# x^T and the forget columns side by side in DRAM, the first eight transfers feeding eight forget blocks k by k

## The chip, the cores and the metric

The kernel runs on one core of a Trainium2 chip. The metric is the device time of one execution in microseconds. The tensor engine is PE (its weight loads PEld), the vector engine DVE, the scalar engine ACT, GpSimd POOL; SP is the queue from which most transfers are issued. KB and MB in the text are 1024 and 1024 x 1024 bytes.

## The reference

One hybrid decoder layer for 256 tokens and 1024 channels. The stage that the change touches is the input projection, and of it the 1024 forget columns; the rest is cut.

```python
proj = jnp.einsum('bsd,dn->bsn', x, w_in)          # 256 x 1024 by 1024 x 9216
hq, hf, hi, hg, mq, mk, mv, gate_logits = jnp.split(proj, offsets, axis=-1)
# hf: columns 1024..2047, 8 heads of 128
o_a = hgrn2_mixer(hq, hf, hi, lb)                  # log_f and k = (1 - lb) * sigmoid(-hf), ...
y_b = moba_attention(rope(mq), rope(mk), mv)       # causal softmax within 256 tokens
mixed = (g_a * (y_a @ w_branch_a) + g_b * (y_b @ w_branch_b)) @ w_out
x = layer_norm(alpha * x + mixed)
return layer_norm(alpha * x + swiglu(x))
```

## The kernel before

**Products.** Every large product is made of three: each operand is split into a high part in the rounded type fp32r and the remainder, and high x high, low x high and high x low are added up in PSUM. `split` (L135) does this with a cast on ACT and a subtraction on DVE; `stage` (L143) does the same to a tile of weights that SP brings from DRAM (`raw` to `wh` and `wl`). A weight tile has 128 x 2048 elements, 1 MB. `plan` (L71) lists all weight tiles in the order in which they are used, and the host lays them into `wts` in that order. `fetch` (L165) takes the next tile and stages as many as three ahead; `prefetch` stages without taking.

**Layouts.** In products with the feature on the partitions ("feat") the weights are the stationary operand, 128 x 128 per k and block, and x^T (1024 channels as 8 pieces k of 128 partitions, 256 tokens) moves: `feat_steps` (L213) issues the three matmuls of 256 columns for each k. A "block" f is 128 columns of the projection; `feat_pair` (L205) takes a tile of two blocks and all eight k and finishes one block after the other. "tok" tiles hold four k and 512 columns.

**Order.** The instructions on PE, DVE and ACT in the block at L255 to L281 go out in the order in which they are written; SP's and those behind the block are ordered by the scheduler, which plays the program through on a model and gives each instruction its place when its inputs and buffers are there. Semaphores and slots are given out by it too: the pool `big` has 12 slots of 8 KB a partition (`slot`), which a tile holds from its first write to its last read; `wraw` has 3 buffers, `whi` and `wlo` 4 each, and in PSUM the pools `mm` and `aux` have 4 banks each.

**The first stage.** L256 to L265: a small activation, a tile of ones, and seven matmuls of ones (`warm`), which PE runs while the first data are under way. L266 to L273: for each k SP brings the x^T piece (128 x 256, 128 KB) and then four blocks' weights of that k (128 x 512, 256 KB, a quarter of a "tok" tile); ACT and DVE split each. `feat_first` (L221) then runs k by k over the four blocks f = 0..3, 12 matmuls a k, into four `aux` banks. L277 brings the tile of blocks 4 and 5 in two halves, L278 computes the lower bounds from the vector `vec`, L279 brings the tile of blocks 6 and 7, and `forget` (L248) evacuates blocks 0 to 3: two sigmoids on ACT (Kt and Fg) and one scaling on DVE. L282 to L287 run blocks 4 to 7 with `feat_pair` out of `mm` banks, one after the other, and evacuate them; the constants `cst` (960 KB) are brought behind the first of these pairs. Then come the query blocks hq (L288), the values hi, the output gates hg and the rest.

Of the kernel before, what the change touches and what calls it, by code (L numbers as in the profile page):

```python
# [10 lines left out]
F32 = mybir.dt.float32  # L11
F32R = mybir.dt.float32r
# [5 lines left out]
P = 128  # L18
T = 256
NT = T // P  # L20
D = 1024
KC = D // P
# [8 lines left out]
NEG = -1e30  # L31
LOOKAHEAD = 3
WARM = 7
EARLY = 4
HOLD_IN = 2
HOLD_DOWN = 3
# [34 lines left out]
def plan():  # L71

    tiles = []

    def add(w, k0, kn, c0, n, held=False):
        tiles.append((w, k0, kn, c0, n, held))

    def feat(w, c0, n):
        for c in range(c0, c0 + n, 256):
            add(w, 0, 8, c, 256)  # L80

    def tok(w, c0, n):
        for c in range(c0, c0 + n, 512):
            add(w, 0, 4, c, 512)
            add(w, 4, 4, c, 512)

    tok("w_in", 1024, 512)
    feat("w_in", 1536, 512)
    feat("w_in", 0, 1024)
    tok("w_in", 2048, 1024)  # L90
    feat("w_in", 3072, 1024)
    feat("w_in", 8192, 1024)
    feat("w_in", 7168, 1024)
    for c in range(2):
        feat("w_in", 5120 + c * 512, 512)
        feat("w_in", 4096 + c * 512, 512)
        tok("w_in", 6144 + c * 512, 512)
    feat("w_branch_a", 0, 1024)
    feat("w_branch_b", 0, 1024)
    for k in range(0, KC, 2):  # L100
        add("w_out", k, 2, 0, 1024)
    for j in range(0, NF, 2):
        add("w_ffn_in", 0, 8, j * P, 256, j < HOLD_IN)
        add("w_ffn_in", 0, 8, FF + j * P, 256, j < HOLD_IN)
    for k in range(0, NF, 2):
        add("w_ffn_down", k, 2, 0, 1024)
    return tiles


@with_exitstack  # L110
def hybrid_layer_kernel(ctx: ExitStack, tc, x, xT, vecs, wts, ln1_w, ln1_b, ln2_w, ln2_b, consts, out):
    nc = tc.nc
    pool = lambda name, bufs, **kw: ctx.enter_context(tc.tile_pool(name=name, bufs=bufs, **kw))
    cp = pool("cp", 1)
    wraw = pool("wraw", 3)
    whi = pool("whi", 4)
    wlo = pool("wlo", 4)
# [3 lines left out]
    mm = pool("mm", 4, space=PSUM)  # L121
    aux = pool("aux", 4, space=PSUM)

    def slot(name, dt=F32):
        return big.tile([P, 2048], dt, tag="s8", name=name)

    def r32(ap):
        return ap.bitcast(F32)


    loads = plan()
    ready = []
    state = {"next": 0}

    def split(dst_h, dst_l, src):  # L135
        nc.scalar.copy(dst_h, src)
        nc.vector.tensor_sub(dst_l, src, r32(dst_h))

    def ks_of(pieces):
        at = np.cumsum((0,) + tuple(pieces))  # L140
        return [slice(int(a), int(b)) for a, b in zip(at[:-1], at[1:])]

    def stage(pieces=None, eng=nc.vector):  # L143
        i = state["next"]
        if i >= len(loads):
            return
        state["next"] += 1
        _, _, k, _, _, held = loads[i]
        src = wts[i].rearrange("p (k c) -> p k c", k=k)
        view = lambda z: z.rearrange("p (k c) -> p k c", k=k)  # L150
        raw = view(wraw.tile([P, 2048], F32, tag="raw", name=f"raw{i}"))
        if held:
            h, l = view(slot(f"wh{i}", F32R)), view(slot(f"wl{i}", F32R))
        else:
            h = view(whi.tile([P, 2048], F32R, tag="h", name=f"wh{i}"))
            l = view(wlo.tile([P, 2048], F32R, tag="l", name=f"wl{i}"))
        for ks in ks_of(pieces or (k,)):
            nc.sync.dma_start(raw[:, ks, :], src[:, ks, :])
            nc.scalar.copy(h[:, ks, :], raw[:, ks, :])  # L159
            yield  # L160
            eng.tensor_sub(l[:, ks, :], raw[:, ks, :], r32(h[:, ks, :]))  # L161
            yield
        ready.append((h, l))

    def fetch(ahead=LOOKAHEAD):  # L165
        while state["next"] < len(loads) and len(ready) < 1 + ahead:
            list(stage())
        return ready.pop(0)
# [3 lines left out]
            list(stage())  # L172


    xTr = slot("xTr").rearrange("p (k t) -> p k t", k=KC)
    xTh = slot("xTh", F32R).rearrange("p (k t) -> p k t", k=KC)
    xTl = slot("xTl", F32R).rearrange("p (k t) -> p k t", k=KC)
    vec = cp.tile([P, 5 * H], F32, tag="vec", name="vec")
    cst = cp.tile([P, C_END], F32, tag="cst", name="cst")
# [25 lines left out]
    def feat_pair(name, ah=None, al=None):  # L205
        ah, al = (xTh, xTl) if ah is None else (ah, al)
        wh, wl = fetch()
        ps = mm.tile([P, 2, T], F32, tag="mm", name=name)
        for f in range(2):
            feat_steps(ps[:, f, :], wh, wl, f, ah, al, range(KC))  # L210
        return ps

    def feat_steps(ps, wh, wl, f, ah, al, ks, k0=0):  # L213
        wcol = slice(f * P, (f + 1) * P)
        for k in ks:
            kk = k0 + k
            nc.tensor.matmul(ps, wh[:, k, wcol], ah[:, kk, :], start=(kk == 0), stop=False)  # L217
            nc.tensor.matmul(ps, wh[:, k, wcol], al[:, kk, :], start=False, stop=False)  # L218
            nc.tensor.matmul(ps, wl[:, k, wcol], ah[:, kk, :], start=False, stop=(kk == KC - 1))  # L219

    def feat_first(pss, tiles):  # L221

        for q, (wh, wl) in enumerate(tiles):
            for k in range(4):
                for f, ps in enumerate(pss):
                    feat_steps(ps, wh, wl, f, xTh, xTl, (k,), 4 * q)

    def tok_chunk(name, evac):
        pss = [mm.tile([P, 512], F32, tag="mm", name=f"{name}_{t}") for t in range(NT)]
# [18 lines left out]
    def forget(h, ps):  # L248
        nc.scalar.activation(Kt[:, :, h, :], by_half(ps), AF.Sigmoid, scale=-1.0)
        nc.scalar.activation(Fg[:, :, h, :], by_half(ps), AF.Sigmoid)  # L250
        nc.vector.tensor_scalar(Fg[:, :, h, :], Fg[:, :, h, :], lb[:, H + h:H + h + 1], lb[:, h:h + 1],
                                op0=ALU.mult, op1=ALU.add)

    ET = mybir.EngineType
    with tc.manual_schedule(engines={ET.PE, ET.DVE, ET.Activation}):  # L255
        act = cp.tile([P, 2], F32, tag="act", name="act")  # L256
        nc.vector.memset(act, 0.0)
        nc.scalar.activation(act[:, 0:1], act[:, 1:2], AF.Exp)
        one = cp.tile([P, P], F32, tag="one", name="one")
        nc.vector.memset(one, 1.0)  # L260
        nc.scalar.copy(ones, one)
        warm = aux.tile([P, P], F32, tag="aux", name="warm")
        for _ in range(WARM):
            nc.tensor.matmul(warm, one, one, start=True, stop=True)
        nc.vector.memset(half, -0.5)  # L265
        for q in range(2):  # L266
            w = stage((1, 1, 1, 1))
            for k in range(4 * q, 4 * q + 4):
                nc.sync.dma_start(xTr[:, k, :], xT[:, k, :])
                split(xTh[:, k, :], xTl[:, k, :], xTr[:, k, :])  # L270
                next(w)
                next(w)
            list(w)  # L273
        nc.sync.dma_start(vec, vecs)
        hf0 = [aux.tile([P, T], F32, tag="aux", name=f"hf0{f}") for f in range(4)]
        feat_first(hf0, [ready.pop(0) for _ in range(2)])
        list(stage((4, 4)))  # L277
        lower_bounds()  # L278
        list(stage())  # L279
        for f in range(4):  # L280
            forget(f, hf0[f])  # L281
    for j in range(2, 4):  # L282
        ps = feat_pair(f"hf{j}")
        if j == 2:
            tc.keep_in_program_order(nc.sync.dma_start(cst, consts))
        for f in range(2):
            forget(2 * j + f, ps[:, f, :])  # L287
    for j in range(4):  # L288
        ps = feat_pair(f"hq{j}")
        sg = sm.tile([P, 2, T], F32, tag="sg", name=f"sgq{j}")  # L290
        nc.scalar.activation(sg, ps, AF.Sigmoid)
        for f in range(2):
            h = 2 * j + f
# [128 lines left out]
    for j in range(4):  # L422
        ps = feat_pair(f"hg{j}")
        sg = sm.tile([P, 2, T], F32, tag="sg", name=f"sgg{j}")
        nc.scalar.activation(sg, ps, AF.Sigmoid)
        for f in range(2):
            h = 2 * j + f
# [87 lines left out]
    for j in range(4):  # L515
        side.step()
        ps = feat_pair(f"za{j}", yah, yal)
# [5 lines left out]
    for j in range(4):  # L523
        ps = feat_pair(f"zb{j}", ybh, ybl)
# [45 lines left out]
    def row_parts(name, widths, n0=0):  # L570
        parts = []
        for i, (p, w) in enumerate(widths):
            parts.append((p.tile([P, w], F32, tag="aux" if p is aux else "mm", name=f"{name}{i}"), n0))
            n0 += w
        return parts
# [57 lines left out]
    pss = [row_parts(f"wo{t}", [(aux, 512)] * 2) for t in range(NT)]  # L633
    wb2 = bcast("wb2", ln2_w, ln2_b)
    with tc.manual_schedule(engines={ET.PE, ET.DVE, ET.Activation}):
        tiles = [(2 * q,) + fetch(0) for q in range(4)]
# [32 lines left out]

    for j in range(EARLY, NF, 2):  # L670
        pg = feat_pair(f"fg{j}", x1h, x1l)
# [4 lines left out]
        i, k = divmod(j, KC)  # L676
        split(ah[i][:, k:k + 2, :], al[i][:, k:k + 2, :], sg)

    pss = [row_parts("wd0", [(aux, 512)] * 2), row_parts("wd1", [(aux, 512), (aux, 256), (mm, 256)])]
    lhs = (lambda kk: ah[kk // KC][:, kk % KC, :], lambda kk: al[kk // KC][:, kk % KC, :])  # L680
    y = slot("y").rearrange("p (t d) -> p t d", t=NT)
    tiles = []
# [8 lines left out]
    layer_norm("n2", 1, pss[1], x1[:, 1, :], wb2, y[:, 1, :], store=out[P:T, :])  # L691


_INS = ['x', 'xT', 'vecs', 'wts', 'ln1_w', 'ln1_b', 'ln2_w', 'ln2_b', 'consts']


# [27 lines left out]
```

## Time and profile before

| | |
|---|---|
| median of 3 runs | 517.9 us (517.75 to 518.09) |
| profiled execution, device time | 517.71 us |
| its span, first to last instruction | 515.7 us |
| mean granted tensor engine clock | 0.997 |
| bytes moved | 91.73 MB, mean 178 GB/s |

The profile is of one execution. A row of the timeline has the start in us from the start of the span, the duration, the engine, the line, the operation, what it writes and reads, and in square brackets the idle time of its engine before it and what ended it. The end of a matmul is modelled, so the pace of PE is read from the starts of consecutive ones and not from the durations. A row of the windows has a stretch, its length, each engine's busy time with the count of its instructions, the granted clock, the busy share of the DMA engines, and what they moved in GB/s. In the chain that ended last, each step is followed back to what released it.

### The profile page before, as it was taken

The page shows a single profiled execution, that of the slowest core. Times are in us where ns is not written, and L with a number is a line of the kernel's source. Part 1 is how long each engine was busy: PE and PEld are TensorE (multiplying, and loading weights), DVE is VectorE, ACT ScalarE, POOL GpSimd, SP SyncE. Part 2 cuts the span into 40 slices and gives each one's busy share as a digit, 9 for nine tenths or more (in the row PEclk, how much of TensorE's full clock was granted, in tenths as well). Part 3 has the DMA queues.
Part 4 walks back from the last instruction along what each step waited for, and adds up shares of the span by engine and source line. Part 5 has one row for each costly group of instructions (what it writes and reads, how often), then busy time and mean ns, then how long its engine had stood idle before and what let it go on. Part 6 is the DMA issues. An engine that isn't in the chain of part 4 may idle for free.

```text
span 515.7 us, 8629 instructions
## 1 busy us (share of the span) xinstructions
PE 506.5 (98%) x3728; PEld 484.8 (94%) x3728; DVE 327.2 (63%) x351; ACT 236.1 (46%) x267; POOL 39.9 (8%) x33
## 2 busy tenths in 40 slices
PE   8999999999999999999999999999999999999994
PEld 7999889999999998998999988999999999988884
DVE  4677799997575444775772899555445454543436
ACT  5695355444354455656442553543443344324300
POOL 0000000000110162353010001000000000000000
PEclk9999999999999999999999999999999999999998
DMA  7988453343424555444575475055554455456002
GB/s 236 354 305 323 167 186 142 128 151 131 164 83 165 168 188 216 165 163 160 179 247 232 163 275 215 5 213 198 192 209 167 165 186 210 174 168 203 39 1 81
DMA packets 15573, 91.73 MB, mean 178 GB/s; under 512 B 1840, under 2 KB 2864, under 8 KB 5552
## 3 DMA queue, kind: packets, MB, share of 16 engines
q1 hardware_dynamic: 14688, 88.04, 47.5%
q0 software_dynamic: 848, 3.15, 1.9%
q8 instruction: 29, 0.48, 0.4%
q14 instruction: 8, 0.07, 0.0%
HBM read 90.13 MB, written 1.05 MB: 177 GB/s over the span
## 4 chain that ended last, share of the span: by engine, by line
PE 98%; DMA 1%; DVE 1%; issue 0%; DVEq 0%; ACT 0%; SPq 0%
PE wd L547 4%; PE wd L546 4%; PE wd L548 4%; PE fu L217 3%; PE fg L218 3%; PE fg L217 3%; PE fg L219 3%; PE fu L218 3%; PE fu L219 3%; PE sc L343 3%; PE hf L219 2%; PE hf L217 2%; PE hf L218 2%; PE mk L219 1%; PE hq L219 1%; PE hq L218 1%
## 5 line engine op out<-in xcount | busy, mean ns | idle before, releaser
L161 DVE TENSOR_TENSOR wl<-raw,wh 128x2048 fp32r<-128x2048 f32 (+2 forms) x88 | 186.6, 2122 | 123.1 <-ACT wh L159 122.7
L159 ACT CAST wh<-raw 128x2048 fp32r<-128x2048 f32 (+2 forms) x88 | 155.8, 1772 | 186.1 <-issue 50.3
L217 PE MATMUL fg<-x1h,wh 128*128 128x256 f32 x144 | 40.8, 284 | 0.0
L217 PE MATMUL fu<-x1h,wh 128*128 128x256 f32 x144 | 40.8, 284 | 0.0
L218 PE MATMUL fg<-x1l,wh 128*128 128x256 f32 x144 | 40.8, 283 | 0.0
L219 PE MATMUL fg<-x1h,wl 128*128 128x256 f32 x144 | 40.8, 283 | 0.0
L218 PE MATMUL fu<-x1l,wh 128*128 128x256 f32 x144 | 40.7, 283 | 0.0
L219 PE MATMUL fu<-x1h,wl 128*128 128x256 f32 x144 | 40.7, 283 | 0.0
L547 PE MATMUL wd<-wl,ah 128*128 128x512 f32 (+1 forms) x110 | 38.2, 348 | 0.0
L546 PE MATMUL wd<-wh,ah 128*128 128x512 f32 (+1 forms) x110 | 38.2, 347 | 0.0
L548 PE MATMUL wd<-wh,al 128*128 128x512 f32 (+1 forms) x110 | 38.1, 347 | 0.0
L218 PEld LDWEIGHTS fg<-x1l,wh 128*128 128x128 f32 x144 | 27.6, 192 | 0.0
L219 PEld LDWEIGHTS fg<-x1h,wl 128*128 128x128 f32 x144 | 27.6, 192 | 0.0
L217 PEld LDWEIGHTS fg<-x1h,wh 128*128 128x128 f32 x144 | 27.6, 192 | 0.0
L218 PEld LDWEIGHTS fu<-x1l,wh 128*128 128x128 f32 x144 | 27.6, 192 | 0.0
L219 PEld LDWEIGHTS fu<-x1h,wl 128*128 128x128 f32 x144 | 27.6, 192 | 0.0
L217 PEld LDWEIGHTS fu<-x1h,wh 128*128 128x128 f32 x144 | 27.6, 192 | 0.0
L546 PEld LDWEIGHTS wd<-wh,ah 128*128 128x128 f32 x110 | 20.8, 189 | 2.7
L548 PEld LDWEIGHTS wd<-wh,al 128*128 128x128 f32 x110 | 20.8, 189 | 2.7
L547 PEld LDWEIGHTS wd<-wl,ah 128*128 128x128 f32 x110 | 20.8, 189 | 2.6
L217 PE MATMUL hf<-xTh,wh 128*128 128x256 f32 x64 | 19.3, 301 | 1.0 <-ACT wh L159 1.0
L219 PE MATMUL hf<-xTh,wl 128*128 128x256 f32 x64 | 19.3, 302 | 0.0
(218 smaller groups left out, 1436.5 us busy)
## 6 DMA issues: line engine op xcount, KB each, us to landing
raw<-in_wts_dram SPq DMA_DIRECT2D x78, 1024.0 KB, 4.8
raw<-in_wts_dram SPq DMA_DIRECT2D x8, 256.0 KB, 5.0
xTr<-in_xT_dram SPq DMA_DIRECT2D x8, 128.0 KB, 4.7
raw<-in_wts_dram SPq DMA_DIRECT2D x2, 512.0 KB, 7.0
xr<-in_x_dram POOLq DMA_DIRECT2D x1, 1024.0 KB, 5.4
wb<-in_ln_w_dram POOLq DMA_DIRECT2D x2, 512.0 KB, 5.7
wb<-in_ln_b_dram POOLq DMA_DIRECT2D x2, 512.0 KB, 7.4
out_dram<-y SPq DMA_DIRECT2D x4, 256.0 KB, 2.1
```

Of the source, the lines that this page charges most:

```text
L159: nc.scalar.copy(h[:, ks, :], raw[:, ks, :])
L161: eng.tensor_sub(l[:, ks, :], raw[:, ks, :], r32(h[:, ks, :]))
L217: nc.tensor.matmul(ps, wh[:, k, wcol], ah[:, kk, :], start=(kk == 0), stop=False)
L218: nc.tensor.matmul(ps, wh[:, k, wcol], al[:, kk, :], start=False, stop=False)
L219: nc.tensor.matmul(ps, wl[:, k, wcol], ah[:, kk, :], start=False, stop=(kk == KC - 1))
L343: nc.tensor.matmul(ps[:, a, :], KL[:, h, :], later(Qt, n, h, 1), start=True, stop=True)
L546: nc.tensor.matmul(ps, lh(kk)[:, ts], wh[:, k, ns], start=(kk == 0), stop=False)
L547: nc.tensor.matmul(ps, lh(kk)[:, ts], wl[:, k, ns], start=False, stop=False)
L548: nc.tensor.matmul(ps, ll(kk)[:, ts], wh[:, k, ns], start=False, stop=(kk == ktot - 1))
```

## The change

x^T and the 1024 forget columns of `w_in` are concatenated on the host into `xw`, of shape 128 x 8 x 1280: for each partition and k, 256 values of x^T and 1024 weights stand in one row. Eight slots of `big` take one k each. SP issues nine transfers: for k = 0 the first 512 columns (x^T and two blocks' weights, 256 KB) and the other 768 (384 KB), then 640 KB for each further k; behind them `vec`. The four forget tiles leave the plan.

ACT and DVE split k by k: x^T, then the weights of all eight blocks of that k (for k = 0 in the parts 256 and 768 columns). The split weights of two k share a `whi` and a `wlo` buffer, so four of each are taken. The new `feat_first` runs, for k = 0 to 5, all eight blocks: first the 16 matmuls with the high weights, then the 8 with the low weights; for k = 0 blocks 0 and 1 go first (four and two), then blocks 2 to 7. `feat_last` runs k = 6 and 7 block by block, so that the blocks end one after the other. The eight banks are the four of `mm` (blocks 0 to 3) and the four of `aux` (4 to 7). Behind it come the lower bounds, one weight tile ahead, the evacuation of blocks 0 to 3, a second tile ahead, and that of 4 to 7; the constants are brought after these in the program. The memset of `one` stands ahead of that of `act`.

```diff
-    tok("w_in", 1024, 512)
-    feat("w_in", 1536, 512)
     feat("w_in", 0, 1024)
...
+    def feat_first(pss, k, wh, wl):
+
+        kk = k % 2
+        for fs in [(0, 1), range(2, 8)] if k == 0 else [range(8)]:
+            for f in fs:
+                wcol = slice(f * P, (f + 1) * P)
+                nc.tensor.matmul(pss[f], wh[:, kk, wcol], xTh[:, k, :], start=(k == 0), stop=False)
+                nc.tensor.matmul(pss[f], wh[:, kk, wcol], xTl[:, k, :], start=False, stop=False)
+            for f in fs:
+                wcol = slice(f * P, (f + 1) * P)
+                nc.tensor.matmul(pss[f], wl[:, kk, wcol], xTh[:, k, :], start=False, stop=False)
+
+    def feat_last(pss, wh, wl):
+
+        for f, ps in enumerate(pss):
+            feat_steps(ps, wh, wl, f, xTh, xTl, (0, 1), KC - 2)
...
+        first = [slot(f"xw{k}")[:, 0:T + D] for k in range(KC)]
+        for k in range(KC):
+            cut = [0, T + FIRST, T + D] if k == 0 else [0, T + D]
+            for c0, c1 in zip(cut[:-1], cut[1:]):
+                nc.sync.dma_start(first[k][:, c0:c1], xw[:, k, c0:c1])
+        nc.sync.dma_start(vec, vecs)
...
-        for q in range(2):
-            w = stage((1, 1, 1, 1))
-            for k in range(4 * q, 4 * q + 4):
-                nc.sync.dma_start(xTr[:, k, :], xT[:, k, :])
-                split(xTh[:, k, :], xTl[:, k, :], xTr[:, k, :])
-                next(w)
-                next(w)
-            list(w)
-        nc.sync.dma_start(vec, vecs)
-        hf0 = [aux.tile([P, T], F32, tag="aux", name=f"hf0{f}") for f in range(4)]
-        feat_first(hf0, [ready.pop(0) for _ in range(2)])
-        list(stage((4, 4)))
+        hf = [p.tile([P, T], F32, tag=tag, name=f"hf{f}")
+              for f, (p, tag) in enumerate([(mm, "mm")] * 4 + [(aux, "aux")] * 4)]
+        for i in range(KC // 2):
+            wh, wl = [p.tile([P, 2048], F32R, tag=tag, name=f"f{tag}{i}").rearrange("p (k c) -> p k c", k=2)
+                      for p, tag in ((whi, "h"), (wlo, "l"))]
+            for k in range(2 * i, 2 * i + 2):
+                cut = [0, FIRST, D] if k == 0 else [0, D]
+                split(xTh[:, k, :], xTl[:, k, :], first[k][:, 0:T])
+                for c0, c1 in zip(cut[:-1], cut[1:]):
+                    split(wh[:, k % 2, c0:c1], wl[:, k % 2, c0:c1], first[k][:, T + c0:T + c1])
+                if k < KC - 2:
+                    feat_first(hf, k, wh, wl)
+        feat_last(hf, wh, wl)
         lower_bounds()
-        list(stage())
-        for f in range(4):
-            forget(f, hf0[f])
-    for j in range(2, 4):
-        ps = feat_pair(f"hf{j}")
-        if j == 2:
-            tc.keep_in_program_order(nc.sync.dma_start(cst, consts))
-        for f in range(2):
-            forget(2 * j + f, ps[:, f, :])
+        prefetch(1)
+        for f in range(8):
+            forget(f, hf[f])
+            if f == 3:
+                prefetch(1)
+    tc.keep_in_program_order(nc.sync.dma_start(cst, consts))
```

More of the change, by code (lines that the diff above doesn't have):

```diff
@@ L33 @@
 WARM = 7
+FIRST = 256
 EARLY = 4
@@ L110, in hybrid_layer_kernel @@
 @with_exitstack
-def hybrid_layer_kernel(ctx: ExitStack, tc, x, xT, vecs, wts, ln1_w, ln1_b, ln2_w, ln2_b, consts, out):
+def hybrid_layer_kernel(ctx: ExitStack, tc, x, xw, vecs, wts, ln1_w, ln1_b, ln2_w, ln2_b, consts, out):
     nc = tc.nc
@@ L172, in prefetch @@
             list(stage())
-    xTr = slot("xTr").rearrange("p (k t) -> p k t", k=KC)
     xTh = slot("xTh", F32R).rearrange("p (k t) -> p k t", k=KC)
@@ L219, in feat_steps @@
             nc.tensor.matmul(ps, wl[:, k, wcol], ah[:, kk, :], start=False, stop=(kk == KC - 1))
[L221 to L226, printed above, removed]
+    def feat_first(pss, k, wh, wl):
[11 more added lines that the diff above has]
+            feat_steps(ps, wh, wl, f, xTh, xTl, (0, 1), KC - 2)
     def tok_chunk(name, evac):
@@ L255, in hybrid_layer_kernel @@
     with tc.manual_schedule(engines={ET.PE, ET.DVE, ET.Activation}):
+        first = [slot(f"xw{k}")[:, 0:T + D] for k in range(KC)]
[4 more added lines that the diff above has]
+        nc.sync.dma_start(vec, vecs)
         act = cp.tile([P, 2], F32, tag="act", name="act")
+        one = cp.tile([P, P], F32, tag="one", name="one")
+        nc.vector.memset(one, 1.0)
         nc.vector.memset(act, 0.0)
         nc.scalar.activation(act[:, 0:1], act[:, 1:2], AF.Exp)
-        one = cp.tile([P, P], F32, tag="one", name="one")
-        nc.vector.memset(one, 1.0)
         nc.scalar.copy(ones, one)
@@ L691, in hybrid_layer_kernel @@
     layer_norm("n2", 1, pss[1], x1[:, 1, :], wb2, y[:, 1, :], store=out[P:T, :])
-_INS = ['x', 'xT', 'vecs', 'wts', 'ln1_w', 'ln1_b', 'ln2_w', 'ln2_b', 'consts']
+_INS = ['x', 'xw', 'vecs', 'wts', 'ln1_w', 'ln1_b', 'ln2_w', 'ln2_b', 'consts']
 def kernel(**inputs):
@@ L703 @@
     given['x'] = x
-    given['xT'] = x.T.reshape(KC, P, T).transpose(1, 0, 2)
+    by_k = lambda z: z.reshape(KC, P, -1).transpose(1, 0, 2)
+    given['xw'] = np.concatenate([by_k(x.T), by_k(given['w_in'][0][:, D:2 * D])], 2)
     given['vecs'] = np.concatenate([given[n].reshape(-1, P) for n in ('lb_logits', 'hgrn_norm_w', 'b_gate')]).T
```

## Prediction, before the result was known

> **What bounds the kernel now.** I read the page first, then what the tensor engine waited for, then the first 31 us of the timeline.
>
> ```profile
> span 515.7 us, 8629 instructions
> PE 506.5 (98%) x3728; PEld 484.8 (94%) x3728; DVE 327.2 (63%) x351; ACT 236.1 (46%) x267; POOL 39.9 (8%) x33
> PE 98%; DMA 1%; DVE 1%; issue 0%; DVEq 0%; ACT 0%; SPq 0%
> ```
>
> The second line is PE's busy time, the third the engines' shares of the chain that ended last: PE is nearly all of it. What PE waited for, in the whole span:
>
> ```profile
> PE warm L264 <- DVE half L265: 1.1, 1, 1.1
> PE hf L217 <- ACT wh L159: 1.0, 1, 1.0
> ```
>
> So PE has two waits, both at the start. An edit of the first stage is worth what it does to the moment at which the 192 hf matmuls (8 blocks x 8 k x 3) are done. The start, in order of time (start, duration, engine):
>
> ```profile
> 0.74 0.37 SPq L269 DMA_DIRECT2D xTr<-in_xT_dram  x1
> 1.09 3.36 PE L264 MATMUL warm<-one 128*128 128x128 f32 x14 [1.09 <-DVE half L265]
> 1.17 0.42 SPq L158 DMA_DIRECT2D raw<-in_wts_dram  x1
> 3.10 0.40 ACT L136 CAST xTh<-xTr 128x256 fp32r<-128x256 f32 x1 [0.67 <-DMA xTr<-in_xT_dram]
> 3.53 0.42 DVE L137 TENSOR_TENSOR xTl<-xTr,xTh 128x256 fp32r<-128x256 f32 x1 [2.49 <-ACT xTh L136]
> 4.80 0.62 ACT L159 CAST wh<-raw 128x512 fp32r<-128x512 f32 x1 [1.30 <-DMA raw<-in_wts_dram]
> 5.33 0.40 ACT L136 CAST xTh<-xTr 128x256 fp32r<-128x256 f32 x1
> 5.47 0.58 PE L217 MATMUL hf<-xTh,wh 128*128 128x256 f32 x1 [1.02 <-ACT wh L159]
> 5.85 0.42 PE L218 MATMUL hf<-xTl,wh 128*128 128x256 f32 x1
> 6.31 0.62 ACT L159 CAST wh<-raw 128x512 fp32r<-128x512 f32 x1 [0.59 <-DMA raw<-in_wts_dram]
> 8.54 0.62 ACT L159 CAST wh<-raw 128x512 fp32r<-128x512 f32 x1 [1.31 <-DMA raw<-in_wts_dram]
> ...
> 10.21 0.41 PE L219 MATMUL hf<-xTh,wl 128*128 128x256 f32 x1
> 10.42 0.36 PE L217 MATMUL hf<-xTh,wh 128*128 128x256 f32 x1
> 10.62 0.27 PE L218 MATMUL hf<-xTl,wh 128*128 128x256 f32 x1
> 10.73 0.28 PE L219 MATMUL hf<-xTh,wl 128*128 128x256 f32 x1
> ...
> 25.36 0.28 PE L218 MATMUL hf<-xTl,wh 128*128 128x256 f32 x1
> 25.59 0.39 PE L219 MATMUL hf<-xTh,wl 128*128 128x256 f32 x1
> ...
> 31.20 0.28 PE L217 MATMUL hq<-xTh,wh 128*128 128x256 f32 x1
> ```
>
> The first x^T piece (128 KB) is cast at 3.10, the first weight piece (256 KB) at 4.80, PE starts at 5.47. Until 10.4 matmuls follow each other every 0.213 us, from 10.62 on every 0.12: the clock rises 5.15 us after the dense work began, although the granted clock below reads 1.00 on both sides. At 25.4 one matmul comes 0.11 late; the next stage begins at 31.20. PE in the two parts (us, busy and count, granted clock, DMA share, GB/s):
>
> ```profile
> 5.40:10.61 5.21, 5.14 (x22) 1.00 0.98 308
> 10.61:31.19 20.58, 20.58 (x172) 1.00 0.92 335
> ```
>
> Two of the 172 reach over the border, so 22 + 170. The pitch of the fast part is (20.58 - 0.11) / 170 = 0.1204 us.
>
> **The change, part by part.** The same 192 matmuls with the same operands run in another order, and the two 1 MB tiles of f = 4..7 no longer come as weight tiles: 5 MB arrive either way before hq's. So no PE work is removed, and only three moments can move: PE's start, the clock's rise, and waits.
>
> *When the data land.* Bytes moved up to the moments at which the casts above began (last column GB/s; the line before is x^T's time from issue to landing, the one behind the weight pieces' of the first 9 us):
>
> ```profile
> DMA to landing us min/median/max: 2.3/4.7/5.5
> 0.00:3.05 3.05, 1.96 (x9) 1.96 (x10) 0.23 (x3) 1.67 (x3) 0.20 (x4) 1.00 0.25 82
> 0.00:4.75 4.75, 3.36 (x14) 3.07 (x14) 0.66 (x4) 2.08 (x4) 0.20 (x4) 1.00 0.46 142
> 0.00:6.29 6.29, 4.18 (x17) 3.66 (x17) 1.50 (x6) 3.00 (x6) 0.20 (x4) 1.00 0.57 171
> 0.00:8.52 8.52, 6.41 (x27) 5.89 (x28) 2.71 (x8) 3.93 (x8) 0.20 (x4) 1.00 0.65 191
> DMA to landing us min/median/max: 3.6/5.1/5.7
> ```
>
> Time by rate is 244, 659, 1050 and 1589 KB moved, when 128, 384, 768 and 1152 KB had landed and could be used: 116, 275, 282 and 437 KB were under way behind them. The new order brings 256 KB first (x^T of k = 0 and two blocks' weights), 384 KB next (the other six blocks), then 640 KB for each k. With 116 to 282 KB under way, interpolated between these rows: first part at 3.57 to 4.25 (taken 3.9), second at 5.13 to 5.82 (5.46), k = 1 at 7.7 to 8.4 (8.1). The issue rows bound the first part from outside: 0.74 plus 2.3, the time of 128 KB, is 3.05; plus 3.6, the fastest 256 KB piece, is 4.34.
>
> A page of the Trainium skill, "DMA: Bandwidth & Descriptors", section "Anatomy of one DMA — SWDGE (gpsimd) path", prices a transfer at about 2.0 us and bytes over 436 GB/s, fitted on another issuing path. The 128 KB at 2.3 us agree with it, the 256 KB at 3.6 against its 2.6 do not. By it, an estimate, the first part would land at 3.3, PE would start as soon as the warm-up ends and the sum below would gain 1.3 us.
>
> *PE's start.* Between first landing and first matmul now stand two casts of 256 columns. A cast's successor starts 0.53 after a 0.62 one (4.80, 5.33), so it overlaps by 0.09: 0.31 + 0.40 and the 0.05 from a cast's end to its matmul (4.80 + 0.62 to 5.47) are 0.76. The start is 3.9 + 0.76 = 4.66 in place of 5.47; it cannot be before the warm-up ends at 4.45, and with a landing at 4.34 it is 5.10.
>
> *The first six matmuls.* Two blocks give six at the slow pitch, plus 0.17 that the first one loses (5.47 to 5.85 is 0.38): 1.45 us, to 6.11. The other 18 of k = 0 need the cast of 768 columns, between 0.62 for 512 and
>
> ```profile
> 17.22 1.05 ACT L159 CAST wh<-raw 128x1024 fp32r<-128x1024 f32 x1 [1.96 <-DMA raw<-in_wts_dram]
> 18.30 2.51 DVE L161 TENSOR_TENSOR wl<-raw,wh 128x1024 fp32r<-128x1024 f32 x2 [2.32 <-ACT wh L159]
> 21.32 1.89 ACT L159 CAST wh<-raw 128x2048 fp32r<-128x2048 f32 x1
> 23.23 1.28 ACT L249 ACT_TABLE_LOAD   x1
> 24.52 0.38 ACT L249 ACTIVATE Kt<-hf 128x256 f32<-128x256 f32 x1
> 23.24 2.29 DVE L161 TENSOR_TENSOR wl<-raw,wh 128x2048 fp32r<-128x2048 f32 x1 [0.98 <-ACT wh L159]
> 5.40:31.15 25.75, 25.68 (x192) 25.30 (x192) 3.62 (x12) 1.00 0.93 330
> ```
>
> 1.05 for 1024, so 0.84: ready at 5.46 + 0.89 = 6.35. PE idles 0.24 us there. The 18 take 3.84 at the slow pitch, to 10.2. For k = 1 ACT needs 0.31 + 1.05 after 8.1, so 9.5: 0.7 us to spare. From there PE needs 24 x 0.1204 = 2.89 us a k, while at 330 GB/s (last row) 640 KB take 2.0, ACT 1.4, and DVE 0.42 + 1.25 (half of the 2.51): the data run ahead of PE, and the 0.11 at 25.4 has no cause any more.
>
> *The clock.* No row shows what counts for its rise. Counted from the start of the dense work, as 5.47 to 10.62, it is 4.66 + 5.15 = 9.81. Ends for the range: 6.24 (5.15 after the warm-up matmuls began at 1.09, if the 1.02 us gap was what made it start over) and 5.15 after a new gap. I take 9.81, since the only rise shown lies behind a dense start.
>
> *Sum.* By 9.81 PE has done 6 + (9.81 - 6.35) / 0.213 = 22.2. The rest, 169.8 x 0.1204, ends at 30.25, against 31.20: **0.95 us gained**. With both landings at their early ends (start 4.45, six blocks at 6.02) it is 1.2, with both late (5.10 and 6.71) 0.55. The profiled execution took 517.71 us with 2.0 around the span, 0.2 under the median of the three runs; the sum gives 516.8.
>
> *What I cost at nothing.* The eight evacuations (two sigmoids of 0.38 and one scaling each) now come at the end instead of in two halves. In the last two k's a block ends every 6 x 0.12 = 0.72 us, so the first is done 5.0 us before the stage's end and its bank, which hq's first product takes, is free after some 0.8; cover 4 us. hq's first weights are behind 5 MB and the small vector: 6 MB by about 23 us at that rate; cast 1.89, table load 1.28, difference 2.29, ready before 27, against a need at 30.3. The second tile is cast behind the fourth block's sigmoids, at 28 to 30, difference to 32.5, needed at 36. Without that cover each late us would be a us. SP issues ten transfers in place of twenty ahead of hq's; none waits behind another's tile, since each k has its own slot. Order of the memsets: under 0.1 us, inside the warm-up.
>
> **The rivals.**
>
> *The clock rises early.* The gap ahead of the first matmul shrinks from 1.02 to about 0.3 us; if that gap restarted the count, the rise comes near 6.24. Then k = 0 is through at 6.35 + 18 x 0.1204 = 8.5, PE waits for k = 1 until 9.5, and 168 x 0.1204 ends at 29.7: 1.5 gained, **516.2**; with the earliest landing 1.8, without any wait 2.45. For it: the warm-up alone had 3.36 us of matmuls and then the gap. Against: they did not raise it themselves. The Trainium skill, "TensorE: Matmul & The Clock Gate", Part 1, has a free-running window of about 3.4 us whose activity decides. One such window ahead of 10.62 is 7.2, and the wait for k = 1 makes the end the same; the trace shows one rise and no window.
>
> *The clock stands at 10.62* whatever PE does: 26 done by then, 166 x 0.1204 ends at 30.6, 0.6 gained, **517.1**. For it: four executions lie within 0.4 us. Against: nothing ties it to that moment.
>
> *The second part is late.* A weight piece of the first 9 us took up to 5.7 us from issue; 1.17 + 5.7 = 6.87. The six blocks then start at 7.76, 1.65 us after PE went idle; a gap of 1.02 already stood before a full 5.15 us of slow clock. So the rise is at 12.91, 30 done by then, 162 x 0.1204 ends at 32.4: 1.2 lost, **518.9**. It decides from a gap of about 1 us, a second part after 6.3. For it: the 437 KB under way at 8.5, and more transfers queued at once. Against: rows of 3 and 5 KB instead of 1 and 2, and fewer issues. Below it the start is only delayed; nothing is lost.
>
> **How the numbers follow.** Forecast 0.36, its own range 516.3 to 517.3; early clock 0.28; clock fixed 0.13; second part late 0.20; 0.03 for a wait further on. No change is told from 0.2%, 1.0 us of 517.9. Faster: nearly half of the forecast's share (its 0.95 is close to the bound) and nearly all of the early clock, 0.44. Slower: most of the late part and the 0.03, 0.17. Within: 0.39. The range 515.4 to 518.9 leaves out an early clock without the wait and half of the late part.
>
> **What would show it.** First hf matmul near 4.7, a gap of 0.2 before the third block, pitch 0.213 until about 9.8, hq's first matmul at 30.3, no other wait of PE. A rise near 6 to 7 with a wait for k = 1 is the first rival; a gap over 1 us and a rise past 12 the last. I am wrong altogether if hq's first weights are late, or if PE, which now waits nowhere behind 5.47, waits in a later stage whose order the scheduler has changed.

## The result, and the profile after

The changed kernel took 516.32 us (median of 20 runs, 515.32 to 518.94) against 517.65 us of the kernel before in the same set (median of 20, 516.60 to 518.72). The ratio is 0.9978, 95% interval 0.9968 to 0.9987: 1.1 us faster, 0.7 to 1.7 (the medians alone differ by 1.3). The profiled execution is the fastest of the 20: 515.32 us with a span of 513.3, against 517.71 and 515.7 before. What its PE waited for:

```profile
PE warm L279 <- DVE half L280: 1.1, 1, 1.1
PE hf L225 <- ACT fh L135: 0.7, 1, 0.7
```

There are still two waits and both are at the start; the second is now one for the weights of k = 1. The start of that execution, in order of time (start, duration, engine; `fh` and `fl` are the split forget weights):

```profile
1.06 3.35 PE L279 MATMUL warm<-one 128*128 128x128 f32 x14 [1.06 <-DVE half L280]
3.42 0.41 ACT L135 CAST xTh<-xw 128x256 fp32r<-128x256 f32 x1 [0.99 <-DMA xw<-in_xw_dram]
3.73 0.40 ACT L135 CAST fh<-xw 128x256 fp32r<-128x256 f32 x1
4.18 0.58 PE L225 MATMUL hf<-xTh,fh 128*128 128x256 f32 x1
4.47 0.83 ACT L135 CAST fh<-xw 128x768 fp32r<-128x768 f32 x1 [0.34 <-DMA xw<-in_xw_dram]
4.56 0.34 PE L226 MATMUL hf<-xTl,fh 128*128 128x256 f32 x1
4.74 0.28 PE L225 MATMUL hf<-xTh,fh 128*128 128x256 f32 x1
4.86 0.28 PE L226 MATMUL hf<-xTl,fh 128*128 128x256 f32 x1
...
6.88 0.88 PE L229 MATMUL hf<-xTh,fl 128*128 128x256 f32 x6
7.03 0.41 ACT L135 CAST xTh<-xw 128x256 fp32r<-128x256 f32 x1 [1.74 <-DMA xw<-in_xw_dram]
7.35 1.04 ACT L135 CAST fh<-xw 128x1024 fp32r<-128x1024 f32 x1
8.44 0.38 PE L225 MATMUL hf<-xTh,fh 128*128 128x256 f32 x1 [0.67 <-ACT fh L135]
...
28.68 0.28 PE L215 MATMUL hq<-xTh,wh 128*128 128x256 f32 x1
```

The first part is cast at 3.42 and PE starts 0.76 us later, at 4.18 in place of 5.47. From the third hf matmul on they follow every 0.12 us, but for a stop of 0.2 us ahead of the third block: the clock rose near 4.6, where before it rose at 10.62. PE is through with k = 0 by 7.8, waits for k = 1 until 8.44, and hq begins at 28.68 in place of 31.20. Those 2.52 us are the difference of the two profiled executions but for 0.1; from hq's first matmul on both take nearly the same (517.71 - 31.20 = 486.5, 515.32 - 28.68 = 486.6). So what an execution gains or loses is read from the moment at which hq begins, and of this number every profile below has its own.

Bytes moved by the moments for which the rows of before are shown in the prediction (last column, GB/s):

```profile
0.00:3.05 3.05, 1.99 (x9) 1.99 (x10) 0.18 (x3) 1.67 (x3) 0.20 (x4) 1.00 0.37 111
0.00:4.75 4.75, 3.69 (x17) 3.63 (x18) 0.95 (x5) 2.67 (x6) 0.20 (x4) 1.00 0.56 198
0.00:8.52 8.52, 6.79 (x39) 6.35 (x39) 2.43 (x8) 4.57 (x8) 0.20 (x4) 1.00 0.76 279
```

Against 82, 142 and 191 before: by 8.5 us nearly half as much again has come.

### The profile page after: what moved, and what is told of

It reads as the page before. It is cut to its first block, busy times and chain, and to the rows that moved or that the text cites. A ratio compares the mean times of both kernels' runs of the same rounds, so it can differ in the third digit from the quotient of the medians.

```text
span 513.3 us, 8602 instructions
## 1 busy us (share of the span) xinstructions
PE 504.3 (98%) x3728; PEld 482.9 (94%) x3728; DVE 327.2 (64%) x349; ACT 236.0 (46%) x265; POOL 39.7 (8%) x33
## 4 chain that ended last, share of the span: by engine, by line
PE 97%; DMA 1%; DVE 1%; ACT 0%; issue 0%; SPq 0%; DVEq 0%
PE wd L560 4%; PE wd L559 4%; PE wd L561 4%; PE fg L215 3%; PE fg L216 3%; PE fu L215 3%; PE fu L216 3%; PE fg L217 3%; PE fu L217 3%; PE sc L356 3%; PE mk L217 1%; PE hq L217 1%; PE hq L216 1%; PE hq L215 1%; PE zb L216 1%; PE ga L216 1%
## 5 line engine op out<-in xcount | busy, mean ns | idle before, releaser
L160 DVE TENSOR_TENSOR wl<-raw,wh 128x2048 fp32r<-128x2048 f32 x77 | 176.3, 2292 | 116.4 <-ACT wh L158 116.2
L158 ACT CAST wh<-raw 128x2048 fp32r<-128x2048 f32 x77 | 146.8, 1909 | 180.7 <-issue 50.6
L217 PE MATMUL za<-yah,wl 128*128 128x256 f32 x64 | 18.5, 288 | 0.0
L216 PE MATMUL za<-yal,wh 128*128 128x256 f32 x64 | 18.4, 288 | 0.0
```

## The experiments

Two questions were open after the result: what makes the changed kernel faster, and why its runs spread over 3.6 us when those of before spread over 2.1. The theories named in the expectations are "closed gap" (PE no longer pauses between the warm-up and hf, so the clock rises earlier), "earlier start" (the first products begin earlier, the clock behind them), "landing" (longer rows and fewer transfers bring the data earlier), "eight blocks" (more work for each k) and "elsewhere" (later stages). All times are against the kernel before, run in the same set; they are medians of 4 to 12 runs, but for one single execution.

### Where the gain does not come from: both kernels with a long warm-up

```diff
-WARM = 7
+WARM = 24
```

> The kernel before with 24 warm-up matmuls, which keep PE busy to about 8.5 to 10 us, so that the first products begin with the clock up and the data there. Both start theories: the start is late by 3 to 4.5 us and the clock is no longer an issue; hf ends near 32.5, 0.5 to 2 us slower than before, the spread of the times smaller than that of before.

> The changed kernel with the same 24 warm-up matmuls, so that start and clock are the same as in the run before with 24. 'Earlier start' and 'closed gap': the two agree within 0.3 us, since nothing but the start and the clock differs. 'Elsewhere' (the order of evacuation, the transfers behind, the scheduler's order of the later stages): the changed kernel is still 1.0 to 1.4 us faster than the kernel before with 24.

The kernel before with 24 came to 1.0016 (1.0007 to 1.0024) of before, the changed one with 24 to 1.0017 (1.0008 to 1.0026). The medians, 518.33 and 518.44, agree within about 0.1 us. These are the warm-up, the first hf and the first hq matmul of the kernel before with 24:

```profile
1.09 7.27 PE L264 MATMUL warm<-one 128*128 128x128 f32 x48 [1.09 <-DVE half L265]
8.12 0.36 PE L217 MATMUL hf<-xTh,wh 128*128 128x256 f32 x1
31.55 0.28 PE L217 MATMUL hq<-xTh,wh 128*128 128x256 f32 x1
```

And these the first hf and the first hq matmul of the changed kernel with 24:

```profile
8.22 0.36 PE L225 MATMUL hf<-xTh,fh 128*128 128x256 f32 x1
31.34 0.28 PE L215 MATMUL hq<-xTh,wh 128*128 128x256 f32 x1
```

With hf begun near 8.2 and the clock up, nothing measurable is left of the change's gain: "elsewhere" falls. Evacuation, order of weights and the scheduler's later stages are worth nothing that these times show.

### The gap between warm-up and hf

```diff
-WARM = 7
+WARM = 9
```

> The kernel before with nine warm-up matmuls in place of seven, so that the tensor engine is busy until about 5.4 us and the gap of 1.02 us ahead of the first hf matmul is closed; nothing else differs. Theory 'closed gap' (the change gains because PE no longer pauses between the warm-up and the first products, so that the clock rises earlier): the clock rises before 7.5 us, the k = 2 data then hold PE for about 0.8 us, and the kernel is 1.3 to 1.8 us faster than before. Theory 'earlier start' (the gain is that the first products begin 1.3 us earlier, the clock rising some 5 us after them either way): rise near 10.6, no difference beyond 0.4 us. Theory 'elsewhere': no difference.

Measured 1.0001 (0.9992 to 1.001): no difference. In the profile the gap is down to 0.33 us and the clock still rises at 10.4:

```profile
1.09 4.21 PE L264 MATMUL warm<-one 128*128 128x128 f32 x18 [1.09 <-DVE half L265]
5.63 0.58 PE L217 MATMUL hf<-xTh,wh 128*128 128x256 f32 x1 [0.33 <-ACT wh L159]
...
10.36 0.32 PE L219 MATMUL hf<-xTh,wl 128*128 128x256 f32 x1
10.52 0.28 PE L217 MATMUL hf<-xTh,wh 128*128 128x256 f32 x1
```

Up to 5.3 us PE has the same work in this execution and in that with 24 warm-ups. But here the 18 entries take 4.21 us, one every 0.23, and there 48 take 7.27, which at 0.23 would be 11. Counted in windows of the warm-up alone (length, PE busy and count), the kernel with 24 has

```profile
3.00:4.00 1.00, 1.00 (x6) 1.00 (x6) 1.00 0.70 211
5.00:6.00 1.00, 1.00 (x12) 1.00 (x11) 1.00 0.98 303
```

so its clock rose between 4 and 5. The same work before it, and a rise near 4.7 in one execution and at 10.4 in the other: the moment is no function of what the kernel does alone.

The unchanged time does not settle "closed gap", though, since the old order has an end that the clock does not move. For blocks 6 and 7 PE needs the low part of their weights, which DVE finishes at 25.53 in the kernel before (23.24 + 2.29, a row shown in the prediction). The load of these weights into PE waited for it; one row each of the kernel before, of its second profile (next section) and of the kernel with 24 warm-ups:

```profile
25.59 0.19 PEld L219 LDWEIGHTS hf<-xTh,wl 128*128 128x128 f32 x1 [0.15 <-DVE wl L161]
24.96 0.19 PEld L219 LDWEIGHTS hf<-xTh,wl 128*128 128x128 f32 x1 [0.15 <-DVE wl L161]
25.93 0.19 PEld L219 LDWEIGHTS hf<-xTh,wl 128*128 128x128 f32 x1 [0.21 <-DVE wl L161]
```

The waits are small, but they say what hq follows:

| profile of the old order | clock up near | first cast of the tile of blocks 4 and 5 | low weights of blocks 6 and 7 done | hq begins |
|---|---|---|---|---|
| kernel before | 10.6 | 17.22 | 25.53 | 31.20 |
| kernel before, second profile | 9.3 | 16.58 | 24.91 | 30.58 |
| nine warm-ups | 10.4 | 17.13 | 25.44 | 31.11 |
| 24 warm-ups | 4.7 | 17.56 | 25.87 | 31.55 |

In all four hq begins 5.67 to 5.68 us after these weights are done and 13.98 to 14.00 after that first cast, which waited for its data (the row at 17.22 in the prediction); between them lie the splits of two tiles and the lower bounds, one behind the other. The clock rises anywhere between 4.7 and 10.6. So in these profiles the stage ends when the tile of blocks 4 and 5 has landed plus a constant, and an earlier clock alone could not have moved it.

> The changed kernel without the warm-up matmuls; nothing else differs. 'Earlier start': hf begins near 4.2 as in the changed kernel, the clock rises some 5 us later (9.3), hf ends near 29.7, so the kernel stays 1.0 to 1.5 us faster than before and within 1.2 us of the changed kernel. 'Closed gap': the first products are the warm-up, the rise comes no earlier than 7.6 and the gain over before falls to 0 to 0.7 us.

(The edit is `WARM = 0` in the changed kernel.) Measured 0.9985 (0.9976 to 0.9994), 0.8 us faster than before (0.3 to 1.2), with no warm-up at all; in the profile, of its fastest run, hf begins at 4.46, the clock is up at 7.4 and hq begins at 29.36. Neither forecast holds as it stands: the rise is earlier than both gave, and 0.8 lies between their ranges. But the new order keeps a gain where there is no gap to close, so a closed gap is not needed for it. Whether a closed gap adds to the gain is not settled.

### The clock in further executions

> The kernel before once more, for a second look at its clock. 'Free window': the rise can lie during the warm-up (3.7 to 4.5) or, if not there, at 7.2 to 10.7; it need not be 10.62 again. 'Fixed lag' or 'fixed moment': 10.62 within 0.1.

> The changed kernel once more, unaltered, as the control of this set and a second look at where the clock rises. 'Free window' (the clock rises at the end of a stretch of about 3.4 us in which PE was busy for some 0.77 of it or more, and where the stretches lie differs from execution to execution): hf from 4.2, rise somewhere between 3.7 and 7.2, 0.7 to 1.6 us faster than before. 'Fixed lag' (5.15 us after the first hf matmul): rise at 9.3.

The kernel before, unaltered, took 517.11 us in the profiled execution, with hq at 30.58, and its clock rose at 9.26:

```profile
9.05 0.39 PE L217 MATMUL hf<-xTh,wh 128*128 128x256 f32 x1
9.26 0.29 PE L218 MATMUL hf<-xTl,wh 128*128 128x256 f32 x1
9.39 0.28 PE L219 MATMUL hf<-xTh,wl 128*128 128x256 f32 x1
```

The changed kernel, unaltered, came to 0.9986 (0.9977 to 0.9995); its profiled execution took 517.19 us:

```profile
4.50 0.58 PE L225 MATMUL hf<-xTh,fh 128*128 128x256 f32 x1
...
6.02 0.48 PE L225 MATMUL hf<-xTh,fh 128*128 128x256 f32 x1
6.33 0.28 PE L226 MATMUL hf<-xTl,fh 128*128 128x256 f32 x1
6.45 0.27 PE L225 MATMUL hf<-xTh,fh 128*128 128x256 f32 x1
...
8.87 0.40 ACT L135 CAST xTh<-xw 128x256 fp32r<-128x256 f32 x1 [2.90 <-DMA xw<-in_xw_dram]
10.27 0.39 PE L225 MATMUL hf<-xTh,fh 128*128 128x256 f32 x1 [1.76 <-ACT fh L135]
...
30.52 0.28 PE L215 MATMUL hq<-xTh,wh 128*128 128x256 f32 x1
```

The clock rose near 6.2, "fixed lag" falls, hf began 0.3 us later than in the first profile, and yet hq began 1.84 us later: k = 1 landed at 8.87 in place of 7.03, and PE stood still for 1.76 us with the clock up. From the first matmul of k = 1 to hq it is 20.24 us in the one execution and 20.25 in the other, the 168 matmuls of seven k at 0.1204; in three further profiles of the new order in which PE waited for k = 1 it is 20.26 to 20.29. With an early clock the new stage ends with k = 1's arrival and a constant.

The Trainium skill, "TensorE: Matmul & The Clock Gate", Part 1, says that the clock is released at the end of a free-running window of about 3.4 us in which PE was busy. Most profiles agree: the 3.4 us ahead of 9.26 and of 10.62 are dense, and the 3.4 us ahead of those hold a gap of about 1 us; in the run without warm-up the 3.4 us ahead of the rise at 7.4 were idle until 4.46 and PE was busy in 2.95 of 3.41. One does not fit by itself: with nine warm-ups the 3.4 us ahead of 7.0 were busy in 3.08 of 3.41, and the clock rose only at 10.4. It fits if the slow first matmuls are counted as partly idle (three there start 0.35 to 0.38 after the one before them instead of 0.213, one in the other run): an estimate then gives 0.77 busy against 0.82. So a window of this kind is argued, and what it counts is not shown.

### Half of the change: rows and transfers, with four blocks

```diff
-    tok("w_in", 1024, 512)
     feat("w_in", 1536, 512)
...
-                nc.sync.dma_start(xTr[:, k, :], xT[:, k, :])
-                split(xTh[:, k, :], xTl[:, k, :], xTr[:, k, :])
+                first = slot(f"xw{k}")[:, 0:T + 512]
+                nc.sync.dma_start(first, xw[:, k, :])
+                split(xTh[:, k, :], xTl[:, k, :], first[:, 0:T])
+                split(wh[:, k % 4, :], wl[:, k % 4, :], first[:, T:T + 512])
```

> Half of the change: x^T and four blocks' weights of a k lie in one DRAM row (3 KB) and come in one transfer of 384 KB, eight transfers in place of sixteen; four blocks a k, the tiles of the other four and the evacuation stay as before. 'Landing' (the gain is that fewer transfers with longer rows land earlier): first landing near 3.8, start near 4.8, so 0.4 to 0.9 us faster than before. 'Eight blocks' (the gain is that PE has twice the work for a k, so that it does not wait for data once the clock is up): no more than 0.3 us.

Measured 1.0177 (1.0164 to 1.0191), 9 us slower, and not for either theory's reason. SP's queue shows it:

```profile
0.74 0.37 SPq L269 DMA_DIRECT2D xw<-in_xw_dram  x1
1.17 0.42 SPq L273 DMA_DIRECT2D vec<-in_vecs_dram  x1
1.64 1.85 SPq L157 DMA_DIRECT2D raw<-in_wts_dram  x4
3.53 8.25 SPq L269 DMA_DIRECT2D xw<-in_xw_dram  x7
```

The order of PE, DVE and ACT is written out, SP's is the scheduler's, and it put four transfers of later weight tiles ahead of k = 1; PE waited 7.8 us for it. In the changed kernel the nine transfers are written ahead of everything else. Mended in this way (all eight ahead of the first memset):

> The half of the change once more, now with its eight transfers of 384 KB (rows of 3 KB) written ahead of everything, as the changed kernel has its nine: four blocks a k, the other four blocks, the weights' order and the evacuation as before. 'Landing': first landing near 3.9, start near 4.9, 0.4 to 1.2 us faster than before, most of the whole change's gain. 'Eight blocks': with twelve matmuls a k PE waits for k = 1 and 2 once the clock is up, and no more than 0.4 us are gained.

Measured 0.9980 (0.9967 to 0.9993): as much as the whole change. Its profiled execution, 515.53 us with hq at 29.02:

```profile
4.42 0.40 ACT L135 CAST xTh<-xw 128x256 fp32r<-128x256 f32 x1 [2.00 <-DMA xw<-in_xw_dram]
...
6.36 0.41 ACT L135 CAST xTh<-xw 128x256 fp32r<-128x256 f32 x1
...
12.80 1.05 ACT L158 CAST wh<-raw 128x1024 fp32r<-128x1024 f32 x1 [0.58 <-DMA raw<-in_wts_dram]
...
18.82 2.29 DVE L160 TENSOR_TENSOR wl<-raw,wh 128x2048 fp32r<-128x2048 f32 x1 [0.98 <-ACT wh L158]
```

Its hf began at 5.40, hardly before the 5.47 of the kernel before, and it waited 1.2 us in all ahead of and in its first products. But k = 2 is there at 6.36, where the weights of k = 2 came at 8.54 before, and with the clock up in its first products PE needs 1.44 us a k and finds each k in place, where "eight blocks" expected waits. The tiles behind come earlier too: the first cast of the tile of blocks 4 and 5 is at 12.80 in place of 17.22, and the low weights of blocks 6 and 7 are done at 21.11 (18.82 + 2.29), 2.4 us before the first matmul with them at 23.50. The end that held the old order is gone. So this half, without the eight blocks side by side and without an earlier start in this execution, brings the gain: "landing" holds, though in a wider sense than I gave it, for all the k and the tiles behind them and not the first alone. Six of its twelve runs took 515.5 to 515.7 us and six 517.1 to 518.2; the profile is of one of the first six, and what held the others is not on record. Longer rows, half as many transfers and their place ahead of everything come together in this run; which of them counts was not tried. Whether the eight blocks add anything is not told apart by these runs.

### The cut of k = 0, and a later start

```diff
-            cut = [0, T + FIRST, T + D] if k == 0 else [0, T + D]
+            cut = [0, T + D]
...
-        for fs in [(0, 1), range(2, 8)] if k == 0 else [range(8)]:
+        for fs in [range(8)]:
```

(and the splits of k = 0 uncut in the same way)

> The changed kernel with k = 0 uncut: one transfer of 640 KB, one cast of 1024 weights, all eight blocks at once as for the other k. 'Earlier start': landing near 4.5, start near 5.9, 1.7 us after the changed kernel's, of which its two later pauses (0.2 and 0.7 us) take some back; so 0.8 to 1.4 us slower than the changed kernel and within 0.4 us of before. 'Closed gap' or 'elsewhere': within 0.4 us of the changed kernel.

Measured 0.9999 (0.9987 to 1.001): within 0.4 us of before, as "earlier start" expected, and 0.7 us behind the changed kernel of the same set (0.9986), with intervals that overlap. Five of its twelve runs took 516.0 to 516.3 us and the others 517.3 to 518.9; the profile is of one with 517.31. In it the first cast is at 4.77, hf begins at 6.18, the clock rises at 9.1 and hq begins at 30.57:

```profile
4.77 0.40 ACT L135 CAST xTh<-xw 128x256 fp32r<-128x256 f32 x1 [2.35 <-DMA xw<-in_xw_dram]
6.34 0.41 ACT L135 CAST xTh<-xw 128x256 fp32r<-128x256 f32 x1 [0.22 <-DMA xw<-in_xw_dram]
...
8.90 0.36 PE L225 MATMUL hf<-xTh,fh 128*128 128x256 f32 x1
9.10 0.28 PE L226 MATMUL hf<-xTl,fh 128*128 128x256 f32 x1
```

> The changed kernel with nine warm-up matmuls, which hold the first hf matmul back to 4.8 (clock up during the warm-up) to 5.5 us (not). 'Earlier start': the start is about that of the kernel before, and most of the gain is gone: 0 to 0.6 us faster than before. 'Closed gap': unchanged, 1.0 to 1.5 us faster.

(`WARM = 9` in the changed kernel.) Measured 0.9975 (0.9966 to 0.9984): nothing lost, where "earlier start" expected most of the gain to go. hf began at 4.92 in its profile, 0.7 us later than in the first profile, found no wait for k = 1, and hq began at 28.90. A start delayed by some tenths is taken out of the wait for k = 1; one delayed by 2 us, as in the profile without the cut, is not; there the clock rose late as well.

### The wait for k = 1

```diff
-                cut = [0, FIRST, D] if k == 0 else [0, D]
+                cut = [0, FIRST, D] if k < 2 else [0, D]
...
-        for fs in [(0, 1), range(2, 8)] if k == 0 else [range(8)]:
+        for fs in [(0, 1), range(2, 8)] if k < 2 else [range(8)]:
```

> The changed kernel with k = 1 split and multiplied in two parts as k = 0 is (256 weight columns, then 768); the transfers are the same. The wait for k = 1 (0.7, 0.3 and 1.8 us in three executions of the changed order) becomes shorter by up to 0.64 us, the difference of a cast of 1024 and one of 256 columns. If that wait is what is left of the early clock's gain: 0.2 to 0.6 us faster than the changed kernel. If the late clock hides it: no difference.

> The changed kernel with k = 1 cut and nine warm-up matmuls, the version that I expect to beat both: hf from 4.9 with the clock up by 7.2 at the latest and little or no wait for k = 1, 1.3 to 1.9 us faster than before.

Measured 0.9963 (0.9950 to 0.9976) with seven warm-ups and 0.9961 (0.9947 to 0.9975) with nine: 1.9 and 2.0 us faster than before, a little more than expected. In the first one's profile, of the slowest of its seven runs, k = 1 landed as late as in the second profile of the changed kernel:

```profile
8.73 0.40 ACT L135 CAST xTh<-xw 128x256 fp32r<-128x256 f32 x1 [2.73 <-DMA xw<-in_xw_dram]
...
9.50 0.39 PE L225 MATMUL hf<-xTh,fh 128*128 128x256 f32 x1 [1.03 <-ACT fh L135]
```

From landing to matmul it is 0.77 us where it was 1.40 (8.87 to 10.27): the 0.63 us that the shorter cast was to give. Both beat the kernel before beyond doubt; against the changed kernel they are 0.8 us ahead, but the intervals overlap, there are only seven and six runs, and the unaltered changed kernel was not timed in that set, so that step is seen in the profile and not settled by the times.

## Why the prediction came out

**The sign and the size** were right: 0.95 us forecast, 1.1 measured (0.7 to 1.7). That the size came so near is luck. The forecast has the clock at 9.81 and no wait behind k = 0; the two profiles of the changed kernel have it near 4.6 and 6.2, waits of 0.67 and 1.76 us for k = 1, and an hq that begins 2.5 and 0.7 us before that of the kernel before. The terms erred against each other, and the mechanism of the sum is not what the executions show.

**Landing and start.** The term from first landing to first matmul, 0.76 us, is what was measured (3.42 to 4.18). In the seven profiles with these nine transfers the first part, taken at 3.9, was cast at 3.42 to 4.00 (mean 3.8); the second, taken at 5.46, at 4.47 to 5.17 (4.8); k = 1, taken at 8.1, at 6.98 to 8.87 (7.8). The second was expected too late, and the range for k = 1, 7.7 to 8.4, was too narrow. (The upper end 5.82 of the second works out at 5.79 from the rows.) The figures came from rows of 1 and 2 KB; the new rows moved 279 GB/s by 8.52 instead of 191. The bound "not before the warm-up ends at 4.45" was false: hf began at 4.18, since the end of a matmul row, 1.06 + 3.35 here, is modelled and PE takes the next one earlier.

**The clock** is the step that failed: "I take 9.81, since the only rise shown lies behind a dense start". One rise was read as a lag. The profiles show about 4.6 and 6.2 for the changed kernel, 10.62 and 9.26 for the one before, and two for the same PE work that differ by over 5 us. The rival "the clock rises early" had the mechanism of both profiles: early rise, then a wait for k = 1, then 168 matmuls. Its wait of 1.0 us stands between the measured 0.67 and 1.76, and its 516.2 between 515.3 and 517.2. The forecast had no wait behind k = 0; both profiles have one. "The clock stands at 10.62" fell with the first profile.

**The wait at 25.4** was put down as 0.11 us that "has no cause any more". That it would go was right, but it was more than 0.11 us: it was the end on which the old order hung. Without its going, an earlier start and an earlier clock would have found the weights of blocks 6 and 7 no earlier.

**The late second part** was seen in its milder form: not the second part but k = 1 came late, and it cost 1.84 us between two profiles without making the clock start over.

**What I cost at nothing** cost next to nothing: from hq's first matmul on the profiles take 486.6 to 486.7 us with the new order of the whole stage and 486.5 with the old one. hq's first weights were cast at 19.95 and their difference was done by 24.2, over 4 us ahead of the need at 28.68; the runs with 24 warm-ups show no later stage that lost or won more.

```profile
19.95 1.91 ACT L158 CAST wh<-raw 128x2048 fp32r<-128x2048 f32 x1
21.89 2.29 DVE L160 TENSOR_TENSOR wl<-raw,wh 128x2048 fp32r<-128x2048 f32 x1 [1.12 <-ACT wh L158]
```

**Still open.** How often the clock rises early in the kernel before is not known, since the timed runs leave no trace; of four profiles with its order of data three rose late (one of them with nine warm-ups) and one early (with 24). The times say this much: of the 98 runs of the kernel before in the four sets none is below 516.5 us, which by the 486.5 above is an hq at 30.0, and of the 31 runs of the unaltered changed kernel 13 are. How much of the 1.1 us is the mean of the clock's moments and how much is data found in place is not split into numbers, and why a good part of the changed kernel's runs take 517 us and more is known for one alone, the second profile with its late k = 1.

## What to carry to other kernels

A stage in which PE is fed at the pace of the transfers is decided by when each piece is usable and by when the clock rises, and not by the first matmul's start: look for the wait behind the first piece. A wait of 0.1 us can mark the end on which a whole stage hangs: ask what PE would find there if it came earlier, and compare several profiles to see what the end of the stage follows. One profile shows one moment of the clock; take a second one of the same kernel before a lag is read from it. Where an order is written out for some engines only, write the transfers that must come first ahead of everything, since the queue that is left to the scheduler may put others between them.

## What the runs showed of the hardware that was not expected

With the first transfer cut in two, the one behind it came later. With k = 0 in one piece, k = 1 followed it after 1.57 us (4.77 to 6.34). With the same 640 KB in pieces of 256 and 384 KB, k = 1 followed the second piece after 2.56 us in the first profile (4.47 to 7.03) and 3.74 in the second (5.13 to 8.87); over the seven profiles with the cut it is 2.07 to 3.74, and k = 1 was never cast before 6.98. PE still starts earlier with the cut and has k = 0 to work on; by the medians the cut is worth 0.4 us in the set of the uncut run, which its intervals do not settle. Why the following transfer is late was not tried.

The granted clock reads 1.00 on all window rows of these starts, while the pitch of the matmuls is 0.213 us before the rise and 0.12 behind it: the rise is to be read from the starts of consecutive matmuls.
